# Hybrid layer: zb, o and the mLSTM merge gates by seven products of halves

## The chip, the cores and the metric

The kernel runs on one core of a Trainium2 chip. Its time is the device time of one execution in microseconds (us); the number used is the median of three runs. Engines are called by the profile's names: PE (TensorE, matmuls), ACT (ScalarE), DVE (VectorE), POOL (GpSimd) and SP (SyncE, which issues most DMAs); PEld is PE loading weights.

## The reference, cut to what matters

Two blocks run one after the other on x of 512 tokens by 1024 features, in fp32. The first block (half an FFN, a mixer, half an FFN, a norm) is not touched. The second block is a hybrid layer:

```
h = rms_norm(x, norm_pre_g)
proj = h @ w_in                      # u_a, z_a, q, k, v, o, z_b, gates, g_a, g_b: 1024 columns each, but gates
q, k = silu(depthwise_conv([q, k]))
hb = mlstm_forward(q, k, v) + mlstm_backward(q, k, v)      # 4 heads of 256
y_b = rms_norm_per_head(hb) * sigmoid(o) * silu(z_b)
y_a = (multiscale_pool(u_a) @ pool_mix) * silu(z_a)
merged = sigmoid(g_a + b_merge[0]) * (y_a @ w_proj_pool) \
       + sigmoid(g_b + b_merge[1]) * (y_b @ w_proj_mlstm)
out = x + rms_norm(merged @ w_out, norm_post_g)
```

## The kernel before, in words

All activations are kept transposed: x is eight tiles of 128 features by 512 tokens. To keep fp32 accuracy each operand is held as two parts, hi (a cast by ACT to the fast fp32 format, line 108 for a loaded chunk of weights `raw`, line 177 for anything else) and lo (the rest, a DVE subtraction, lines 109 and 178). One product is three matmuls, hi·hi, hi·lo and lo·hi (`mm3`, lines 125 to 127). Weights come as one stream of chunks of 128 x 1024 in the order of their use: SP loads a chunk into a ring of three `raw` tiles, and its `whi` and `wlo` parts go to rings of three each. A tile of 128 output features is 8 x 3 = 24 matmuls of 512 columns and uses one chunk.

In the FFNs most pairs of gate and up tiles are computed another way (`fast`): the 1024 inputs and the 512 tokens are each cut into two halves, and the 2x2 block product is done with seven products of halves instead of eight, as in Winograd's form of Strassen's method. They are called a, b, p, c, d, f and e, and each is 4 x 3 = 12 matmuls of 256 columns. For that the kernel needs sums of x's halves (`x_sums`: sa, sb, then sxh, sxl) and of the weights' halves: blocks r1, r2, r3 and r4, some of them summed by a DMA that accumulates (POOL's queue), the others by two DVE additions (r<-r,r), and all split into hi and lo. Product a needs r1's parts, p and c those of r2, d and f those of r3, e those of r4. The partial results are put together on the way from the banks fx, fy and fz by ACT copies (fs, fr) and DVE additions (ft, fu). `chain` order: the last two products (f, e) of one pair are placed among the first (a, b) of the next.

The second block runs in this order on PE: the gates' tile; per head q, k, the scores sT and the numerators num, with the values V before heads 0 and 2; eight zb tiles (silu, line 1055) and then eight o tiles (sigmoid, line 1061), whose DVE product lies in `gate`; the transposes hT of the normed heads hb, which DVE multiplies into gate (line 1074), split as ybh and ybl; the merge of branch b (line 1083), in which each mg tile (the gate of the merge, `mgt`) is followed by a pr tile (the projection of y_b); then branch a's u_a, z_a and pooling, its merge, and the output projection. After the last head POOL multiplies the eight x tiles by the row factors r3bc (line 1047), and DVE works out the head norms hrs from hss (lines 202 to 210) and scales hb (line 1067).

What sets the order: the kernel's code gives each operation in sequence, and when the program is built a scheduler fixes each engine's instruction order from it. On the chip each engine goes through its list in order and an instruction waits until its operands, and the tile that it writes, are free. So a late operand holds up everything behind it on its engine. `tc.issue_after` holds the two additions of a fast pair behind a marked instruction. Tiles with one tag share a ring: `big` is a ring of 18 tiles (gate, ybh, ybl and more), and V and PK of the heads and `n2` of the later stages have memory of their own.

Of the kernel before, what the change touches and what calls it, by code (L numbers as in the profile page):

```python
# [44 lines left out]
def kernel(  # L45
# [21 lines left out]
    def wtmp(name, shape=None):  # L67
        return tp.tile(shape or [P, T], F32, tag="w", name=name, bufs=4)
# [155 lines left out]

    def ffn(gname, fstd, ah, al, stats, evac, first=None):
        with tc.tile_pool(name="hp", bufs=2 * max(FPH)) as hp:
# [17 lines left out]

            H = [slice(0, 256), slice(256, 512)]
            sx = []

            def x_sums(k):
                xa, xb = wtmp("xa"), wtmp("xb")
                act.activation(xa, x[k], AF.Copy, scale=vcol(gname, k))  # L250
                act.activation(xb, x[k + 4], AF.Copy, scale=vcol(gname, k + 4))
                h = hp.tile([P, 4, 256], F32R, tag="sx", name="sxh", bufs=8)
                l = hp.tile([P, 4, 256], F32R, tag="sx", name="sxl", bufs=8)
                sa, sb = vtmp("sa"), vtmp("sb")
                dve.tensor_sub(sa[:, H[0]], xa[:, H[0]], xa[:, H[1]])
                dve.tensor_add(sa[:, H[1]], sa[:, H[0]], xb[:, H[1]])
                dve.tensor_sub(sb[:, H[0]], xa[:, H[1]], xb[:, H[1]])
                dve.tensor_sub(sb[:, H[1]], xb[:, H[0]], sa[:, H[1]])
                for j, s in ((0, sa), (2, sb)):
                    split_into(*[m[:, j:j + 2].rearrange("p a b -> p (a b)") for m in (h, l)], s, None)  # L260
                sx.append((h, l))

            for f in range(fstd):
                if first and f == 0:
                    g, u = first
                else:
                    g = gemm_t(tl, ah, al, "g")
                    u = gemm_t(tl, ah, al, "u")
                if rbc is None:
                    rbc = row_bcast(rsqrt_small(sums(stats()), 1.0 / D, "r"))  # L270
                for k in range(KT // 2):
                    if k * fstd // 4 == f:
                        x_sums(k)
                ins = hidden(g, u)
                if f == fstd - 2:
                    marks = [ins]

            def fast():  # L280

                wg, wu = wst[state["n"]], wst[state["n"] + 1]
                state["n"] += 2
                A, B = slice(0, T), slice(T, 2 * T)
                r3 = wp.tile([P, 1024], F32, tag="raw", name="r3", bufs=3)
                r1 = hp.tile([P, 1024], F32, tag="r1", name="r1", bufs=2)
                r2 = hp.tile([P, 1024], F32, tag="r2", name="r2", bufs=2)
                r4 = half("r4")
                nc.sync.dma_start(r3[:, A], wg[:, A])
                nc.gpsimd.dma_start(r3[:, A], wu[:, A], accum_op=ALU.add)  # L290
                nc.sync.dma_start(r4, wu[:, B])
                nc.sync.dma_start(r1[:, A], wg[:, A])
                nc.sync.dma_start(r2[:, B], wu[:, A])
                nc.gpsimd.dma_start(r2[:, B], wu[:, B], accum_op=ALU.add)
                nc.sync.dma_start(r2[:, A], wg[:, B])
                with tc.issue_after(marks[-1].ins):
                    dve.tensor_add(r1[:, B], r3[:, A], r4)
                    dve.tensor_add(r3[:, B], r1[:, B], r2[:, A])
                w = {}
                for r, names in ((r1, "ab"), (r2, "pc"), (r3, "df"), (r4, "e")):  # L300
                    if r is r4:
                        hi, lo = half("hi4", F32R), half("lo4", F32R)
                    else:
                        hi = wp.tile([P, 1024], F32R, tag="whi", name="whi")
                        lo = wp.tile([P, 1024], F32R, tag="wlo", name="wlo")
                    split_into(hi, lo, r, None)
                    for n, c in zip(names, (A, B)):
                        w[n] = hi[:, c], lo[:, c]

                def prod(o, n, xo, start):  # L310
                    for k in range(4):
                        ks = slice(k * P, (k + 1) * P)
                        if isinstance(xo, int):
                            xh, xl = sx[k][0][:, xo], sx[k][1][:, xo]
                        else:
                            p, i = xo
                            xh, xl = ah[k + 4 * p][:, H[i]], al[k + 4 * p][:, H[i]]
                        wh, wl = w[n]
                        for j, (m, v) in enumerate(((wh, xh), (wh, xl), (wl, xh))):
                            pe.matmul(o[:, :256], m[:, ks], v, start=start and k == 0 and j == 0,  # L320
                                      stop=k == 3 and j == 2, skip_group_check=not start)

                X, Y, Z = bank("fx", "mm"), bank("fy", "mm"), bank("fz")
                s1, s2 = wtmp("fs"), wtmp("fr")
                t, u = vtmp("ft"), vtmp("fu")
                prod(X, "a", (0, 0), True)
                act.copy(s1[:, H[0]], X[:, :256])
                yield
                prod(Y, "b", 1, True)
                act.copy(s1[:, H[1]], Y[:, :256])  # L330
                yield
                prod(Z, "p", (1, 0), True)
                dve.tensor_add(t[:, H[0]], Z[:, :256], s1[:, H[0]])
                prod(X, "c", 0, False)
                act.copy(s2[:, H[0]], X[:, :256])
                prod(Y, "d", 2, False)
                dve.tensor_sub(u[:, H[1]], Y[:, :256], s2[:, H[0]])
                yield
                prod(X, "f", (1, 1), False)
                marks.append(dve.tensor_sub(t[:, H[1]], X[:, :256], s1[:, H[1]]))  # L340
                yield
                prod(Y, "e", 3, False)
                dve.tensor_sub(u[:, H[0]], Y[:, :256], s1[:, H[0]])
                hidden(t, u)
                yield

            f0 = fstd
            for ph, n in enumerate(FPH):
                last = None
                for _ in range(f0, n):  # L350
                    g = fast()
                    for i in range(3):
                        next(g)
                        if last and i < 2:
                            next(last)
                    last = g
                for _ in range(2):
                    next(last)
# [543 lines left out]
    big = lambda name, dt=F32, shape=None: bp_.tile(shape or [P, T], dt, tag="big", name=name)  # L902
    lx = ExitStack()
# [49 lines left out]
    def values2(steps=iter(())):  # L953
        V = [[lp.tile([P, 2, 258], F32R, tag="V", name="V", bufs=2 * NT) for _ in range(2)] for i in range(NT)]
# [28 lines left out]
    hb = [lt(f"hb{i}", shape=[P, 2, 256]) for i in range(8)]  # L983
    hss = mb.tile([P, NT, 4], F32, name="hss")
    for h in range(4):
# [18 lines left out]
        PK = [[lp.tile([P, T], F32R, tag="PK", name="PK", bufs=10) for _ in range(2)] for _ in range(5)]  # L1004
# [16 lines left out]
        for t in range(NT):  # L1021
# [19 lines left out]
            sq = mv.tile([P, 256], F32, tag="hsq", name="hsq")  # L1041
            act.activation(sq, hv, AF.Square, accum_out=hss[:, t, h:h + 1])
# [5 lines left out]


    gate = []  # L1050
    for c in range(KT):
        o = gemm_t(tl, ah, al, "zb")
        g = big("gate")
        dve.tensor_mul(g, o, rbc)
        act.activation(g, g, AF.Silu)
        gate.append(g)
    for c in range(KT):
        o = gemm_t(tl, ah, al, "o")
        t = wtmp("og")
        dve.tensor_mul(t, o, rbc)  # L1060
        act.activation(t, t, AF.Sigmoid)
        dve.tensor_mul(gate[c], gate[c], t)
# [17 lines left out]
    np2 = ctx.enter_context(tc.tile_pool(name="n2", bufs=26))  # L1080
    nn = lambda name, dt=F32, shape=None: np2.tile(shape or [P, T], dt, tag="n", name=name)


    def merged(yh, yl, br, into):
        for c in range(KT):
            o = gemm_t(tl, ah, al, "mg")
            t = wtmp("mgt")
            dve.tensor_mul(t, o, rbc)
            act.activation(t, t, AF.Sigmoid, bias=vcol("bmerge", 8 * br + c))
            o = gemm_t(tl, yh, yl, "pr")  # L1090
            into(c, t, o)

    mm = []

    def into_b(c, t, o):
        m = nn("mm")
        dve.tensor_mul(m, t, o)
        mm.append(m)

    merged(yh, yl, 1, into_b)  # L1100


# [61 lines left out]
    merged(yh, yl, 0, into_a)  # L1164
# [59 lines left out]
def _stream(i):  # L1224
# [71 lines left out]
    put(t_tiles(zb))  # L1296
    put(t_tiles(o))
# [73 lines left out]
```

## Time and profile before

| what | value |
|---|---|
| median of three runs | 1617.14 us (1617.07 to 1618.35) |
| the profiled execution's own time | 1618.24 us |
| its span, first to last instruction | 1616.5 us |
| PE busy | 1598.9 us (99%) |
| DVE, ACT, POOL busy | 1087.0, 749.2, 136.6 us |
| mean granted TensorE clock | 0.999 of full speed |
| zb tiles, o tiles on PE | 1184.2 to 1241.2 us, 1241.2 to 1284.7 us |
| merge of branch b on PE | 1287.4 to 1376 us |

The profile is of one execution. Busy time is the time in which an engine had at least one instruction at work; matmuls are pipelined, so that one of 0.39 us may be followed by the next after 0.23. The time from one start to the next, the pitch, is what a matmul costs in a full stream. The first zb matmuls are placed among the last head's work, so the zb stretch is longer than eight tiles alone.

### The profile page before, as it was taken

The page shows a single profiled execution, that of the slowest core. Times are in us where ns is not written, and L with a number is a line of the kernel's source. Part 1 is how long each engine was busy: PE and PEld are TensorE (multiplying, and loading weights), DVE is VectorE, ACT ScalarE, POOL GpSimd, SP SyncE. Part 2 cuts the span into 40 slices and gives each one's busy share as a digit, 9 for nine tenths or more (in the row PEclk, how much of TensorE's full clock was granted, in tenths as well). Part 3 has the DMA queues.
Part 4 walks back from the last instruction along what each step waited for, and adds up shares of the span by engine and source line. Part 5 has one row for each costly group of instructions (what it writes and reads, how often), then busy time and mean ns, then how long its engine had stood idle before and what let it go on. Part 6 is the DMA issues. An engine that isn't in the chain of part 4 may idle for free.

```text
span 1616.5 us, 23488 instructions
## 1 busy us (share of the span) xinstructions
PE 1598.9 (99%) x9050; PEld 1388.9 (86%) x9050; DVE 1087.0 (67%) x1902; ACT 749.2 (46%) x1173; POOL 136.6 (8%) x253
## 2 busy tenths in 40 slices
PE   8999999999999999999999999999999999999997
PEld 6989989987788898898998998888888888888886
DVE  6866866876364866875686778798677543566454
ACT  6533535545244554653352556577573322333341
POOL 0101101000100110110110100011002000110000
PEclk9999999999999999999999999999999999999999
DMA  7545745432142100674574642222222232323231
GB/s 237 142 141 136 188 127 148 133 103 92 53 130 87 34 25 27 151 176 130 138 181 125 162 119 91 92 66 66 65 66 92 78 104 94 100 93 104 92 118 53
DMA packets 68320, 176.22 MB, mean 109 GB/s; under 512 B 7664, under 2 KB 7984, under 8 KB 68208
## 3 DMA queue, kind: packets, MB, share of 16 engines
q1 hardware_dynamic: 56592, 153.38, 29.2%
q0 software_dynamic: 11040, 20.45, 8.0%
q8 instruction: 71, 1.16, 0.3%
q10 hardware_dynamic: 576, 0.89, 0.2%
q14 instruction: 41, 0.34, 0.1%
HBM read 171.55 MB, written 2.10 MB: 107 GB/s over the span
## 4 chain that ended last, share of the span: by engine, by line
PE 94%; DVE 2%; issue 1%; ACT 1%; DMA 0%; POOL 0%; SPq 0%; DVEq 0%; ACTq 0%; POOLq 0%
PE fx L320 10%; PE fy L320 10%; PE dn L127 5%; PE dn L125 5%; PE dn L126 5%; PE fz L320 3%; PE pv L777 2%; PE gn L125 2%; PE gn L126 2%; PE gn L127 2%; PE g L127 2%; PE g L125 2%; PE mg L125 2%; PE mg L126 2%; PE mg L127 2%; PE pr L125 2%
## 5 line engine op out<-in xcount | busy, mean ns | idle before, releaser
L108 ACT CAST whi<-raw 128x1024 fp32r<-128x1024 f32 x179 | 188.0, 1051 | 354.6 <-issue 147.8
L109 DVE TENSOR_TENSOR wlo<-raw,whi 128x1024 fp32r<-128x1024 f32 x179 | 223.5, 1249 | 69.2 <-ACT whi L108 67.5
L177 ACT CAST whi<-r 128x1024 fp32r<-128x1024 f32 x111 | 116.4, 1051 | 115.9 <-PE dn L126 52.8
L178 DVE TENSOR_TENSOR wlo<-r,whi 128x1024 fp32r<-128x1024 f32 x111 | 135.2, 1219 | 15.5 <-ACT whi L177 15.3
L127 PE MATMUL dn<-hdh,wlo 128*128 128x512 f32 x352 | 137.0, 389 | 0.0
L126 PE MATMUL dn<-hdl,whi 128*128 128x512 f32 x352 | 137.0, 389 | 0.0
L125 PE MATMUL dn<-hdh,whi 128*128 128x512 f32 x352 | 136.7, 389 | 0.0
L320 PE MATMUL fx<-xh,whi 128*128 128x256 f32 x296 | 84.3, 285 | 0.0
L320 PE MATMUL fy<-sxh,whi 128*128 128x256 f32 x296 | 83.8, 283 | 0.0
L320 PE MATMUL fy<-sxl,whi 128*128 128x256 f32 x296 | 83.8, 283 | 0.0
L320 PE MATMUL fy<-sxh,wlo 128*128 128x256 f32 x296 | 83.8, 283 | 0.0
L320 PE MATMUL fx<-xh,wlo 128*128 128x256 f32 x296 | 83.7, 283 | 0.0
L320 PE MATMUL fx<-xl,whi 128*128 128x256 f32 x296 | 83.7, 283 | 0.0
L126 PEld LDWEIGHTS dn<-hdl,whi 128*128 128x128 f32 x352 | 66.1, 188 | 13.9 <-DVE hdl L178 0.3
L127 PEld LDWEIGHTS dn<-hdh,wlo 128*128 128x128 f32 x352 | 66.1, 188 | 13.5
L125 PEld LDWEIGHTS dn<-hdh,whi 128*128 128x128 f32 x352 | 66.1, 188 | 13.2
L364 DVE TENSOR_TENSOR dnr<-dn,rbc 128x512 f32<-128x512 f32 x48 | 33.1, 690 | 58.4 <-PE dn L127 58.3
L125 PE MATMUL g<-xh,whi 128*128 128x512 f32 x152 | 61.1, 402 | 6.8 <-ACT xh L180 6.8
L126 PE MATMUL g<-xl,whi 128*128 128x512 f32 x152 | 60.8, 400 | 0.5 <-DVE xl L181 0.5
L127 PE MATMUL g<-xh,wlo 128*128 128x512 f32 x152 | 60.5, 398 | 0.0
L125 PE MATMUL gn<-whi,xh 128*128 128x512 f32 (+1 forms) x160 | 59.1, 370 | 0.0
L127 PE MATMUL gn<-whi,xl 128*128 128x512 f32 (+1 forms) x160 | 59.0, 368 | 0.0
(497 smaller groups left out, 4581.5 us busy)
## 6 DMA issues: line engine op xcount, KB each, us to landing
raw<-in_dram SPq DMA_DIRECT2D x192, 512.0 KB, 3.4
r<-in_dram SPq DMA_DIRECT2D x185, 256.0 KB, 3.6
r<-in_dram POOLq DMA_DIRECT2D x74, 256.0 KB, 4.6
x<-in_dram SPq DMA_DIRECT2D x8, 256.0 KB, 6.5
out_dram<-xn SPq DMA_DIRECT2D x8, 256.0 KB, 2.2
post<-in_dram ACTq DMA_DIRECT2D x2, 256.0 KB, 4.0
acc<-kcT POOLq DMA_DIRECT2D x2, 128.0 KB, 3.2
acc<-vcT POOLq DMA_DIRECT2D x2, 128.0 KB, 2.5
```

Of the source, the lines that this page charges most:

```text
L108: act.copy(hi, raw)
L109: dve.tensor_sub(lo, raw, hi.bitcast(F32))
L125: pe.matmul(out, lh, rh, start=start, stop=False)
L126: pe.matmul(out, lh, rl, start=False, stop=False)
L127: pe.matmul(out, ll, rh, start=False, stop=stop)
L177: act.copy(h, src)
L178: dve.tensor_sub(l, src, h.bitcast(F32))
L320: pe.matmul(o[:, :256], m[:, ks], v, start=start and k == 0 and j == 0, stop=k == 3 and j == 2, skip_group_check=not start)
L364: dve.tensor_mul(t, o, rbc)
L777: pe.matmul(o[:, i * 65:(i + 1) * 65], pt[:, q0:q0 + P], vn[kt][:, b, e, :65], start=(kt == 0), stop=(kt == i))
```

## The change

`seven` (the former `fast`), `x_sums` and `chained` become common functions, and the second block uses them: zb and o are taken in pairs (zb tile c with o tile c). Pairs 0 and 1 stay standard, pairs 2 to 7 go by seven products in one chain. In the merge of branch b the eight mg tiles become four pairs by seven products, each a chain of its own, followed by its two pr tiles. `branch_gate` now does silu and sigmoid for a pair at a time. The sums of x for the second block are made beside the first two pairs (eight sx tiles of each part); since they read x, the row broadcast of r3 and POOL's eight multiplications of x move behind the zb/o chain. One ring `n2` of 26 tiles now holds V, hb and PK of the heads and later sx, the merge's r2a and r2b, mm and the rest. The blocks r2a, r2b, r4 and the parts hi4, lo4 of the zb/o chain, and r4 of the merge, are tiles of `big`. The separate tile hsq goes. The weight stream is packed in the new order. The program has 362 more matmul instructions (84 for 48 in each of ten pairs, and two more).

```diff
+    def seven(ah, al, sx, blocks, marks, done):
+        wa, wb = wst[state["n"]], wst[state["n"] + 1]
...
+        r3 = wp.tile([P, 1024], F32, tag="raw", name="r3", bufs=3)
+        r1, r2, r4, low = blocks()
...
+        nc.sync.dma_start(r4, wb[:, B])
...
+        with tc.issue_after(marks[-1].ins):
+            dve.tensor_add(r1[:, B], r3[:, A], r4)
+            dve.tensor_add(r3[:, B], r1[:, B], ra)
...
+    def branch_gate(z, o):
+        g = big("gate")
+        dve.tensor_mul(g, z, rbc)
+        act.activation(g, g, AF.Silu)
+        t = wtmp("og")
+        ins = dve.tensor_mul(t, o, rbc)
+        act.activation(t, t, AF.Sigmoid)
+        dve.tensor_mul(g, g, t)
...
+    def blocks():
+        r1 = wp.tile([P, 1024], F32, tag="raw", name="r1", bufs=3)
+        return r1, (big("r2a"), big("r2b")), big("r4"), lambda: (big("hi4", F32R), big("lo4", F32R))
+
+    def blocks_b():
+        r1 = wp.tile([P, 1024], F32, tag="raw", name="r1", bufs=3)
+        return r1, (nn("r2a"), nn("r2b")), big("r4"), lambda: [
+            wp.tile([P, 1024], F32R, tag=t, name=t)[:, :T] for t in ("whi", "wlo")]
+
+    for c in range(2):
+        z = gemm_t(tl, ah, al, "zb")
+        o = gemm_t(tl, ah, al, "o")
+        for k in (2 * c, 2 * c + 1):
+            sx.append(x_sums(k, "pre2", [[nn(n, F32R).rearrange("p (a b) -> p a b", a=2) for n in ("sxh", "sxl")]
+                                         for _ in range(2)]))
+        marks.append(branch_gate(z, o))
+    chained(seven(ah, al, sx, blocks, marks, branch_gate) for _ in range(2, KT))
 
     r3bc = row_bcast(r3)
     for d in range(KT):
         pool.tensor_mul(x[d], x[d], r3bc)
-    gate = []
-    for c in range(KT):
-        o = gemm_t(tl, ah, al, "zb")
...
-    for c in range(KT):
-        o = gemm_t(tl, ah, al, "o")
...
-    merged(yh, yl, 1, into_b)
+    def gates_b(t, o):
+        c = len(mm)
+        for d, m in ((c, t), (c + 1, o)):
+            g, ins = merge_gate(1, d, m)
+            pr = gemm_t(tl, yh, yl, "pr")
+            m = nn("mm")
+            dve.tensor_mul(m, g, pr)
+            mm.append(m)
+            marks.append(ins)
+
+    for c in range(0, KT, 2):
+        chained([seven(ah, al, sx, blocks_b, marks, gates_b)])
```

How this moves instructions is shown at three places. First ACT behind the last head. Before, the zb tiles' weights are cast between the last squares of the head; here is its list:

```order
912 L1039 ACTIVATE ha<-num,dn 128x256
913 L1042 ACTIVATE hsq,hss<-hb_10303 128x256
914 L218 COPY rbc<-bc 128x512
915 L1039 ACTIVATE ha<-num,dn 128x256
916 L108 CAST whi<-raw 128x1024
917 L1042 ACTIVATE hsq,hss<-hb_10305 128x256
918 L1055 ACTIVATE gate<-gate 128x512
919 L108 CAST whi<-raw 128x1024
```

The same place after, with r_12369 the block r1 of the first seven-product pair and r_12368 its r3:

```order
926 L233 ACTIVATE xb<-x_79,vs 128x512
927 L177 CAST sxh<-sa 128x512
928 L1069 ACT_TABLE_LOAD
929 L1069 ACTIVATE gate<-gate 128x512
930 L177 CAST sxh<-sb 128x512
931 L1072 ACT_TABLE_LOAD
932 L1072 ACTIVATE og<-og 128x512
933 L177 CAST sxh<-sa 128x512
934 L177 CAST whi<-r_12369 128x1024
935 L177 CAST sxh<-sb 128x512
936 L177 CAST whi<-r2a 128x512
937 L177 CAST whi<-r2b 128x512
```

The first cast of a weight now stands behind the sums of x and two loads of a function table. Second DVE from the last o tile on. Before, the list runs from the last og to the first weight of the merge that is split behind the heads:

```order
1549 L1060 TENSOR_TENSOR og<-o,rbc 128x512
1550 L1074 SCALAR_TENSOR_TENSOR gate<-hT,vs,gate 128x512 x2
1551 L1062 TENSOR_TENSOR gate<-gate,og 128x512
1552 L178 TENSOR_TENSOR ybl<-gate,ybh 128x512
...
1563 L1074 SCALAR_TENSOR_TENSOR gate<-hT,vs,gate 128x512
1564 L178 TENSOR_TENSOR ybl<-gate,ybh 128x512
1565 L1088 TENSOR_TENSOR mgt<-mg,rbc 128x512
1566 L178 TENSOR_TENSOR ybl<-gate,ybh 128x512
1567 L109 TENSOR_TENSOR wlo<-raw,whi 128x1024 x2
1568 L1097 TENSOR_TENSOR mm<-mgt,pr 128x512
```

After, with r_13310 the block r1 of the first merge pair, r_13309 its r3 and r_13313 its r4:

```order
1626 L1071 TENSOR_TENSOR og<-fu,rbc 128x512
1627 L1112 SCALAR_TENSOR_TENSOR gate<-hT,vs,gate 128x512 x4
1628 L1073 TENSOR_TENSOR gate<-gate,og 128x512
1629 L1112 SCALAR_TENSOR_TENSOR gate<-hT,vs,gate 128x512
...
1635 L1112 SCALAR_TENSOR_TENSOR gate<-hT,vs,gate 128x512
1636 L178 TENSOR_TENSOR ybl<-gate,ybh 128x512 x5
1637 L259 TENSOR_TENSOR r_13310<-r_13309,r_13313 128x512
1638 L260 TENSOR_TENSOR r_13309<-r_13310,r2a 128x512
1639 L178 TENSOR_TENSOR wlo<-r_13310,whi 128x1024
1640 L178 TENSOR_TENSOR wlo<-r2a,whi 128x512
```

The first mg product is made (mgt) before the last ybl in the one; in the other the weights of the first merge product are added and split behind all ybl. Third ACT in the merge of branch b. Before, a turn of it reads:

```order
949 L1089 ACTIVATE mgt<-mgt,vs 128x512
950 L108 CAST whi<-raw 128x1024 x2
951 L1089 ACTIVATE mgt<-mgt,vs 128x512
952 L108 CAST whi<-raw 128x1024 x2
953 L1089 ACTIVATE mgt<-mgt,vs 128x512
```

After, the second merge pair, with r_13512 its r1, r_13511 its r3, r_13515 its r4 and raw the chunks of the pr tiles:

```order
1019 L1123 ACTIVATE mgt<-mgt,vs 128x512 x2
1020 L177 CAST whi<-r_13512 128x1024
1021 L292 COPY fs<-fx 128x256
1022 L295 COPY fs<-fy 128x256
1023 L177 CAST whi<-r2a 128x512
1024 L177 CAST whi<-r_13511 128x1024
1025 L177 CAST whi<-r_13515 128x512
1026 L177 CAST whi<-r2b 128x512
1027 L108 CAST whi<-raw 128x1024
1028 L300 COPY fr<-fx 128x256
1029 L108 CAST whi<-raw 128x1024
```

The casts of r2a, r3, r4 and r2b stand behind the copies of the results of products a and b (fs).

## Rows read from the trace of the kernel before

**Rows 1.** The page: busy us (share of the span); DMA issues, count, KB each, us to landing.

```profile
PE 1598.9 (99%) x9050; PEld 1388.9 (86%) x9050; DVE 1087.0 (67%) x1902; ACT 749.2 (46%) x1173; POOL 136.6 (8%) x253
...
r<-in_dram SPq DMA_DIRECT2D x185, 256.0 KB, 3.6
```

**Rows 2.** Waits of PE: line, what for; us in total, times, longest.

```profile
PE g L125 <- ACT xh L180: 6.8, 2, 6.5
PE g L126 <- DVE xl L181: 0.5, 1, 0.5
```

**Rows 3.** Windows: stretch and its us; busy us of PE, PEld, DVE, ACT, POOL; clock.

```profile
9.00:12.00 3.00, 2.85 (x7) 1.49 (x5) 1.48 (x3) 1.75 (x3) 0.00 (x0) 1.00 1.05 389
50.00:95.00 45.00, 45.00 (x350) 43.57 (x349) 34.99 (x52) 24.40 (x37) 4.92 (x6) 1.00 0.69 187
1213.00:1241.00 28.00, 28.00 (x128) 23.27 (x128) 24.34 (x37) 9.75 (x16) 11.04 (x8) 1.00 0.26 83
1285.00:1376.00 91.00, 91.00 (x418) 75.48 (x417) 41.23 (x50) 27.39 (x34) 0.15 (x2) 1.00 0.29 93
```

**Rows 4.** Timeline of PE, o tiles' first and last matmul: start, us, instruction.

```profile
1241.16 0.39 PE L125 MATMUL o<-xh,whi 128*128 128x512 f32 x1
...
1284.45 0.40 PE L127 MATMUL o<-xh,wlo 128*128 128x512 f32 x1
1284.69 2.92 PE L1072 MATMUL hT<-ident,hb 128*128 128x128 f32 x24
```

**Rows 5.** Timeline of PE, first product of two neighbouring fast pairs of the FFN.

```profile
73.26 0.28 PE L320 MATMUL fx<-xh,whi 128*128 128x256 f32 x1
...
83.34 0.28 PE L320 MATMUL fx<-xh,whi 128*128 128x256 f32 x1
```

**Rows 6.** Lines by form, ACT from 1184 to 1376: busy us, mean ns; idle before.

```profile
L108 ACT CAST whi<-raw 128x1024 fp32r<-128x1024 f32 x33 | 34.7, 1052 | 97.6 <-issue 55.8 <-PE mg L126 31.3 <-PE zb L126 6.2
L177 ACT CAST ybh<-gate 128x512 fp32r<-128x512 f32 x8 | 4.9, 619 | 3.3 <-DVE gate L1074 3.2
L1039 ACT ACTIVATE ha<-num,dn 128x256 f32<-128x256 f32 x4 | 1.8, 474 | 3.4 <-DVE dn L1036 3.4
L1055 ACT ACT_TABLE_LOAD x1 | 1.3, 1283 | 0.0
```

**Rows 7.** Timeline of ACT, two casts back to back.

```profile
1294.84 1.14 ACT L177 CAST ybh<-gate 128x512 fp32r<-128x512 f32 x2
```

**Rows 8.** Lines by form, DVE from 1184 to 1376.

```profile
L109 DVE TENSOR_TENSOR wlo<-raw,whi 128x1024 fp32r<-128x1024 f32 x32 | 40.2, 1259 | 4.8 <-ACT whi L108 3.8
L1074 DVE SCALAR_TENSOR_TENSOR gate<-hT,vs,gate 128x512 f32<-128x512 f32 x8 | 5.9, 744 | 0.0
L178 DVE TENSOR_TENSOR ybl<-gate,ybh 128x512 fp32r<-128x512 f32 x8 | 5.5, 683 | 0.4 <-ACT ybh L177 0.4
```

**Rows 9.** Timeline of DVE behind the last head, from 1214 to 1226.

```profile
1214.15 0.69 DVE L1054 TENSOR_TENSOR gate<-zb,rbc 128x512 f32<-128x512 f32 x1 [0.32 <-PE zb L127]
1214.76 0.47 DVE L1040 SCALAR_TENSOR_TENSOR hb<-num,dn,ha 128x256 f32<-128x256 f32 x1
1215.62 2.37 DVE L109 TENSOR_TENSOR wlo<-raw,whi 128x1024 fp32r<-128x1024 f32 x1 [0.39 <-ACT whi L108]
1217.91 1.26 DVE L202 TENSOR_SCALAR hrsv<-hss 128x16 f32<-128x16 f32 x1
...
1225.46 0.17 DVE L208 TENSOR_TENSOR hrsq<-hrs 128x16 f32<-128x16 f32 x1
```

**Rows 10.** Line 1047: duration ns min/median/max, first and last start us.

```profile
L1047 POOL TENSOR_TENSOR x<-x,rbc x8: 1287/1297/2286, 1214.4 to 1224.1; 128x512 f32<-128x512 f32 x8
```

**Rows 11.** Timeline of PE at the program's start: first and ninth matmul, and the tenth.

```profile
6.53 0.79 PE L125 MATMUL g<-xh,whi 128*128 128x512 f32 x1 [6.53 <-ACT xh L180]
...
11.24 0.61 PE L127 MATMUL g<-xh,wlo 128*128 128x512 f32 x1
12.15 0.50 PE L125 MATMUL g<-xh,whi 128*128 128x512 f32 x1 [0.29 <-ACT xh L180]
```

More of the change, by code (lines that the diff above doesn't have):

```diff
@@ L225, in ffn, with chained @@
+    def chained(tiles):
+        last = None
+        for g in tiles:
+            for i in range(3):
+                next(g)
+                if last and i < 2:
+                    next(last)
+            last = g
+        for _ in range(2):
+            next(last)
     def ffn(gname, fstd, ah, al, stats, evac, first=None):
@@ L242, in hidden, with sx_tiles @@
                 return ins
-            H = [slice(0, 256), slice(256, 512)]
             sx = []
[L248 to L261, printed above, removed]
+            def sx_tiles():
+                h, l = [hp.tile([P, 4, 256], F32R, tag="sx", name=n, bufs=8) for n in ("sxh", "sxl")]
+                return [(h[:, 2 * j:2 * j + 2], l[:, 2 * j:2 * j + 2]) for j in range(2)]
             for f in range(fstd):
@@ L272, in ffn @@
                     if k * fstd // 4 == f:
-                        x_sums(k)
+                        sx.append(x_sums(k, gname, sx_tiles()))
                 ins = hidden(g, u)
@@ L276, in ffn @@
                     marks = [ins]
[L280 to L285, printed above, removed]
+            def blocks():
                 r1 = hp.tile([P, 1024], F32, tag="r1", name="r1", bufs=2)
                 r2 = hp.tile([P, 1024], F32, tag="r2", name="r2", bufs=2)
[L288 to L345, printed above, removed]
@@ L347, in ffn, with fast @@
+                return r1, (r2,), half("r4"), lambda: (half("hi4", F32R), half("lo4", F32R))
+            def fast():
+                return seven(ah, al, sx, blocks, marks, hidden)
             f0 = fstd
             for ph, n in enumerate(FPH):
[L349 to L356, printed above, removed]
@@ L357, in ffn @@
-                for _ in range(2):
-                    next(last)
+                chained(fast() for _ in range(f0, n))
                 f0 = 0
@@ L953, in values2 @@
     def values2(steps=iter(())):
-        V = [[lp.tile([P, 2, 258], F32R, tag="V", name="V", bufs=2 * NT) for _ in range(2)] for i in range(NT)]
+        V = [[nn("V", F32R, [P, 2, 258]) for _ in range(2)] for i in range(NT)]
         for i in range(NT):
@@ L981, in conv @@
         return split(a, None, "qk", big)
-    hb = [lt(f"hb{i}", shape=[P, 2, 256]) for i in range(8)]
+    hb = [nn(f"hb{i}", shape=[P, 2, 256]) for i in range(8)]
     hss = mb.tile([P, NT, 4], F32, name="hss")
@@ L1003 @@
             Mb.append(o)
-        PK = [[lp.tile([P, T], F32R, tag="PK", name="PK", bufs=10) for _ in range(2)] for _ in range(5)]
+        PK = [[nn("PK", F32R) for _ in range(2)] for _ in range(5)]
         for j in range(NT):
@@ L1079, with merge_gate @@
     lx.close()
[L1080 to L1091, printed above, removed]
-    mm = []
[L1095 to L1098, printed above, removed]
-    merged(yh, yl, 1, into_b)
+    def merge_gate(br, c, o):
+        t = wtmp("mgt")
+        ins = dve.tensor_mul(t, o, rbc)
+        act.activation(t, t, AF.Sigmoid, bias=vcol("bmerge", 8 * br + c))
+        return t, ins
+    mm = []
+    tl = Tiles()
+    def gates_b(t, o):
[9 more added lines that the diff above has]
+        chained([seven(ah, al, sx, blocks_b, marks, gates_b)])
     yh, yl = [], []
@@ L1162, in into_a @@
         act.copy(xn[i][g], o)
-    merged(yh, yl, 0, into_a)
+    for c in range(KT):
+        t, _ = merge_gate(0, c, gemm_t(tl, ah, al, "mg"))
+        into_a(c, t, gemm_t(tl, yh, yl, "pr"))
     gp2 = []
```

94 lines of the change are left out of this document (81 added, 13 removed).

## The prediction

> **What bounds the kernel now.** I read the page first: TensorE is busy for 99% of the span [rows 1]. Then TensorE's waits: two at the start of the program (6.8 us for the first x tiles, 0.5 us), the largest of six groups that sum to under 9 us in 1616.5 [rows 2]. Then the windows of the stretches that the change touches, and of an FFN stretch that already works by seven products: TensorE is busy for the whole of each, and the vector and scalar engines never fill theirs (VectorE 24.34 of 28 us at most) [rows 3]. So a matmul saved is worth its full pitch, but only as long as TensorE's operands are ready without exception, and any late operand shows at once as new time. The question is not the saving but whether the new order still hides the splitting of the weights.
>
> **1. The products: −8.0 us.** A standard pair of tiles is 48 matmuls of 512 columns. The 192 of the o tiles start from 1241.16 to 1284.45, so (1284.45 − 1241.16)/191 = 0.2266 us each [rows 4], 10.88 us a pair. A pair by seven products is 84 matmuls of 256 columns; in the FFN 84 of them start in 83.34 − 73.26 = 10.08 us [rows 5]. Ten pairs (six zb/o, four mg) save 10 × 0.80 = 8.0 us.
>
> **2. The start of the zb/o chain: +7.7 us.** Call T the end of the last head's last num matmul. After it TensorE has only 5 zb and 24 o matmuls left, 29 × 0.2266 = 6.6 us. In before 11 zb and o tiles with plain loads follow there, whose casts run well ahead. In after the first weight that the chain needs, r1 of the first pair, is cast on ScalarE behind the rest of the head and all of x_sums. By the compiled order that is 4 ha and 4 squares with their reads, 4 xa/xb, 8 sxh casts, 3 table loads, 3 gate functions and the cast itself. Back to back an instruction starts about 0.1 us before its predecessor's end (two ybh casts of 0.62 take 1.14 [rows 7]), so by [rows 6], with a square as a ha and an xa as a cast and a little more, this is 8 × 0.4 + 4 × 0.6 + 8 × 0.52 + 3 × 1.28 + 3 × 0.53 + 1.0 = 16.2 us, of which some 2.5 lie before T. The cast ends at T + 13.7, wlo (1.26 us [rows 8]) at T + 15.0. TensorE's queue holds two product matmuls ahead of the one that needs wlo and is empty by T + 7.3: idle 7.7 us. Bounds: 5 (a third table load or some casts slip behind) and 9.
>
> **3. Between the pairs of that chain: +2 us.** After pair n's d product 19 matmuls (2.3 us) stand before the third a of pair n+1, which needs its wlo. That wlo waits on VectorE for fu<-fy,fr, and its cast on ScalarE for fr, behind two table loads (1.28 each) and two functions of the pair before. In the steady state this just fits (wlo at 1.9 to 2.4 us); the first transitions, where ScalarE still works off x_sums, lack 0.3 to 0.9 each. Bounds 0 and 5.
>
> **4. From the chain's end to the first merge pair: +20 us.** This is the largest term. Let E be the last e matmul. TensorE then has the r3 transposes and 32 hT transposes (24 took 2.92 us [rows 4]; about 4 us in all) and five product matmuls; the sixth waits for wlo of r1. VectorE works first through fu, og, 8 scalings of gate by hT, a gate product, 8 ybl. The DMA that loads r4 of the first merge pair waits for the seventh ybl, because their tiles share the ring of 18. Without disturbance the seventh ybl ends at E + 11.5: 1.0 + 8 × 0.67 of hT scalings + 8 × 0.60 of gate product and seven ybl, by [rows 8, 9] (an operation of 0.69 is followed 0.61 later). r4 needs 3.6 us to land [rows 1]. Then r1's add, cast and wlo follow in a row, 0.68 + 1.05 + 1.26: wlo at E + 18.2, idle 18.2 − 4 − 0.6 = 13.6 us.
> It is disturbed, though. GpSimd's eight products x<-x,rbc stood under zb tiles in before; now they start when rbc is copied, about E + 3. In before, while they ran (8 of 1.3 us, one of them 2.29 [rows 10]), a wlo took 2.37 us instead of 1.26, and six VectorE operations of 16 elements a partition took 1.21 to 1.26 us each, where the same ones took 0.17 as soon as GpSimd had ended [rows 9]. The gate<-zb product, one of whose operands is in PSUM, took its usual 0.69 us there. So each SBUF-only operation seems to take turns with a GpSimd product. The gate product and seven ybl are eight such operations, so each costs a GpSimd product and itself, 1.25 + 0.60 = 1.85 us, with the hT scalings beneath: E + 3 + 8 × 1.85 = E + 17.8 for the seventh ybl, wlo at E + 24.4, idle 20 us. I take 20; bounds 10 (r4 landing while other work remains, no turns) and 21. Nothing covers it: in before the hT transposes stood between mg matmuls whose weights were long split, and here every product after them needs this wlo.
>
> **5. Merge pairs 2 to 4: +6 us.** ScalarE's order puts both fs copies, which wait for product b's end, ahead of the cast of r2a, which product p needs. TensorE is then at p before the cast: a and b last 24 × 0.12 = 2.9 us, the copies and the cast end 1.2 us later (a copy of 256 columns taken a little under a ha [rows 6]), and p's third matmul waits another 0.5 for wlo (0.68). Two pr matmuls stand before f and wait some 0.6 for the cast of their raw tile. That is 2.3 a pair and 6.8 for three; in the fourth eight transposes stand in the gaps, −0.9. Bounds 3 and 8. The first merge pair has its casts in order.
>
> **6. The restart after an idle stretch: +2 us.** At the program's start, after 6.5 us without work, nine matmuls fill the time from 6.53 to 12.15 [rows 11], 0.8 of it waits [rows 2]: 0.53 us each instead of 0.2266, 2.8 us lost. The granted clock is shown as 1.00 there [rows 3], the 2.4 GHz level, so the column doesn't explain it. Two long idle stretches cost 0 to 5.6 us if each ends in such a restart; I take 2. The Trainium skill ("TensorE: Matmul & The Clock Gate", section "What's actually happening") says that an idle array runs at 1.2 GHz until it has been busy for a while. By that rule the full price would fall due twice; the rows' slow pitch agrees with it, their clock column doesn't.
>
> What costs nothing: x_sums on VectorE (it lies in term 2's wait for ScalarE), the shared ring n2 (its tiles are free long before), the last head itself (67 matmuls of cover against 70), and both FFNs and the mixer, whose order is unchanged.
>
> **Sum.** −8.0 + 7.7 + 2 + 20 + 6 + 2 = +29.7 against the profiled execution's own 1618.24 us, which lies 1.1 above the median of the three runs (1617.14). On the median this gives 1647 us, +1.8%. All low bounds together: −8 + 5 + 0 + 10 + 3 + 0 = +10 (1627); all high ones: −8 + 9 + 5 + 21 + 8 + 5.6 = +41 (1658).
>
> **The rivals.**
> - Covered splits (faster). In the FFN stretch the same seven products run at 0.120 us with TensorE busy for 45 of 45 us [rows 3, 5], so the form itself needs no wait. If the weights of both new starts were split in time, only term 1 stays: 1609 us. Against it: in the FFN the first pair's split stands under standard tiles still running, here 6.6 us and 4 us of cover face chains of 15 and 18 to 24.
> - GpSimd doesn't hold VectorE up, as ybl works on other data than the small operations seen: term 4 is 13.6, time 1640 to 1641. For it: only one wide operation was caught in the overlap; against it: that one lost 1.1 us.
> - ScalarE sets the pace of the zb/o chain: two table loads, two functions, five casts and three copies are some 8 us of a pair's 10.08, and if their order makes every transition lack 1.6 us, term 3 is 8: 1653.
> - Both idle stretches end in a restart at the full price of the program's start: term 6 is 5.6, time 1651.
>
> **How the numbers follow.** Chances: my forecast 0.5, GpSimd harmless 0.2, ScalarE's pace 0.1, full restart price 0.1, covered splits 0.05, and 0.05 for a mixture in which some cover that I missed takes most of the 30 us away. Two tenths of a per cent, 3.2 us, is what a measurement can tell from no change. Faster: the covered case, 0.05. Same: half of the last, 0.03. Slower: 0.92. The range, 1630 to 1658, leaves out the covered case and the corner in which every term is at its low end.
>
> **What would show it.** In the profile after, TensorE's waits must list some 7 us for wlo once at the first fx of the chain, 10 to 20 us once after the hT transposes, and two to three waits of 0.5 to 1.2 us in each of merge pairs 2 to 4. Between the waits the 256-column pitch must be 0.120. GpSimd's eight products must lie beside the ybl, and a ybl there must take 1.2 us or more. If TensorE stays busy through both places, the forecast is wrong; if the wait after hT is below 14 us, its turn-taking part is.

## The result, and the profile after

The changed kernel takes 1657.42 us, median of four runs (1655.39 to 1659.21), against 1617.74 before: a ratio of 1.0243, 95% interval 1.0227 to 1.0258. The prediction was 1647 in a range of 1630 to 1658. The profiled execution took 1658.11 us with a span of 1656.4, 39.9 more than before; from the last num matmul to the first ua matmul it is 201.7 us where it was 162.6, so 39.1 of the 39.9 lie in the stretch that the change touches.

The page after shows TensorE busy for longer, 1605.2 us, but for 97% of the span instead of the 99% of [rows 1], and the clock column shows for the first time slices under full speed:

```profile
PE 1605.2 (97%) x9410; PEld 1409.2 (85%) x9410; DVE 1139.0 (69%) x2016; ACT 800.6 (48%) x1262; POOL 156.0 (9%) x273
...
PE   8999999999999999999999999999988599999997
...
PEclk9999999999999999999999999999999799999999
```

TensorE's waits, which were under 9 us in the whole program [rows 2], now read as follows (columns as there):

```profile
PE fx L285 <- ACT whi L177: 21.5, 2, 16.0
PE fx L285 <- ACT fr L300: 6.9, 4, 2.6
...
PE fz L285 <- ACT whi L177: 2.9, 3, 1.0
PE pr L125 <- ACT whi L108: 0.9, 2, 0.4
```

The first line is the two starts (5.5 and 16.0 us), the second the transitions of the zb/o chain, the others merge pairs 2 to 4. In the timeline of PE the start of the chain is one gap, and what follows it is slow:

```profile
1219.73 0.39 PE L127 MATMUL o<-xh,wlo 128*128 128x512 f32 x1
1225.58 0.58 PE L285 MATMUL fx<-xh,whi 128*128 128x256 f32 x1 [5.47 <-ACT whi L177]
...
1230.25 0.41 PE L285 MATMUL fy<-sxl,whi 128*128 128x256 f32 x1
1230.47 0.41 PE L285 MATMUL fy<-sxh,wlo 128*128 128x256 f32 x1
...
1230.88 0.28 PE L285 MATMUL fy<-sxl,whi 128*128 128x256 f32 x1
1231.00 0.28 PE L285 MATMUL fy<-sxh,wlo 128*128 128x256 f32 x1
```

Up to 1230.7 the products start 0.21 us apart, then 0.12 as in the FFN [rows 5]. The windows (columns as in [rows 3]) give the reason in the granted clock, at this place and behind the largest gap:

```profile
1218.00:1226.00 8.00, 2.53 (x12) 1.84 (x11) 7.86 (x20) 7.94 (x13) 0.00 (x0) 0.88 0.23 35
1226.00:1230.00 4.00, 4.00 (x19) 3.88 (x19) 4.00 (x6) 2.93 (x6) 0.00 (x0) 0.50 0.40 126
...
1306.00:1322.00 16.00, 0.48 (x2) 0.48 (x3) 13.50 (x14) 4.05 (x7) 10.46 (x7) 0.60 0.10 33
1322.00:1326.00 4.00, 4.00 (x20) 3.88 (x20) 3.06 (x4) 1.83 (x3) 0.00 (x0) 0.50 0.42 131
```

0.50 is the level of 1.2 GHz. VectorE is busy for 13.50 of the 16 us in which TensorE waits there. Its timeline, and GpSimd's products and the ybl by duration (minimum, median, maximum in ns, as in [rows 10]):

```profile
1304.29 1.02 DVE L1073 TENSOR_TENSOR gate<-gate,og 128x512 f32<-128x512 f32 x1
1305.24 0.74 DVE L1112 SCALAR_TENSOR_TENSOR gate<-hT,vs,gate 128x512 f32<-128x512 f32 x1
1305.90 1.09 DVE L178 TENSOR_TENSOR ybl<-gate,ybh 128x512 fp32r<-128x512 f32 x1
...
1307.57 1.08 DVE L178 TENSOR_TENSOR ybl<-gate,ybh 128x512 fp32r<-128x512 f32 x1
...
1310.91 6.70 DVE L178 TENSOR_TENSOR ybl<-gate,ybh 128x512 fp32r<-128x512 f32 x5
1319.69 0.69 DVE L259 TENSOR_TENSOR r<-r,r 128x512 f32<-128x512 f32 x1 [2.08 <-DMA r<-in_dram]
```

```profile
L1100 POOL TENSOR_TENSOR x<-x,rbc x8: 1277/1708/1712, 1303.5 to 1314.8; 128x512 f32<-128x512 f32 x8
L178 DVE TENSOR_TENSOR ybl<-gate,ybh x8: 678/1090/1747, 1305.9 to 1316.9; 128x512 fp32r<-128x512 f32 x8
```

A ybl takes 1.09 us behind a scaling and 1.75 in a row instead of 0.68 [rows 8]; the last, when GpSimd has ended, takes 0.68 again. Either way one ybl follows the other after 1.67 us, about the time of a product on GpSimd, which takes 1.71 us instead of 1.30. The hT scalings, with one operand in PSUM, keep their 0.74. Behind the ybl r1's addition waits another 2.1 us for the block r4.

The table sets the prediction's terms against the trace. A gap is the time from one matmul's start to the next beyond its pitch; the clock's price is the sum, over windows of 1 us, of PE's busy time times what the granted clock lacks to 1.

| term | predicted | measured |
|---|---|---|
| 1 products | -8.0 | -8.8 (66 matmuls from 1251.86 to 1259.57: 0.119 us each, 84 in 10.0 us) |
| 2 start of the chain | +7.7 | 5.6 |
| 3 inside the chain | +2 | 8.2 (2.7, 1.9, 0.7, 2.3, 0.7) |
| 4 behind the chain | +20 | 17.3 (16.2, and 1.1 among the hT) |
| 5 merge pairs 2 to 4 | +6 | 5.3 (2.1, 2.1, 1.1) |
| 6 clock behind gaps | +2 | 8.3 |
| sum | +29.7 | +35.9 of 39.9 |

The 4 us that are left are not traced one by one; steps of 0.1 to 0.3 us, some 3 us in all, are part of them. The 16.7 us of the expectations below count 0.5 of the steps among the hT with the 16.2.

### The profile page after: what moved, and what is told of

It is laid out like the page before. It is cut to its first block, busy times and chain, and to the rows that moved or that the text cites. A ratio compares the mean times of both kernels' runs of the same rounds, so it can differ in the third digit from the quotient of the medians.

```text
span 1656.4 us, 24572 instructions
## 1 busy us (share of the span) xinstructions
PE 1605.2 (97%) x9410; PEld 1409.2 (85%) x9410; DVE 1139.0 (69%) x2016; ACT 800.6 (48%) x1262; POOL 156.0 (9%) x273
## 5 line engine op out<-in xcount | busy, mean ns | idle before, releaser
L178 DVE TENSOR_TENSOR wlo<-r,whi 128x1024 fp32r<-128x1024 f32 x135 | 162.5, 1204 | 24.2 <-ACT whi L177 23.6
L285 PE MATMUL fx<-xh,whi 128*128 128x256 f32 x376 | 110.0, 293 | 28.5 <-ACT whi L177 21.5
L285 PE MATMUL fy<-sxh,whi 128*128 128x256 f32 x392 | 111.7, 285 | 0.0
L285 PE MATMUL fy<-sxl,whi 128*128 128x256 f32 x392 | 111.6, 285 | 0.0
L285 PE MATMUL fy<-sxh,wlo 128*128 128x256 f32 x392 | 111.4, 284 | 0.0
L285 PEld LDWEIGHTS fx<-xh,whi 128*128 128x128 f32 x376 | 74.2, 197 | 33.1 <-ACT whi L177 22.4
L285 PEld LDWEIGHTS fy<-sxh,whi 128*128 128x128 f32 x392 | 76.2, 194 | 0.0
L285 PEld LDWEIGHTS fy<-sxl,whi 128*128 128x128 f32 x392 | 76.0, 194 | 0.0
L285 PEld LDWEIGHTS fy<-sxh,wlo 128*128 128x128 f32 x392 | 75.8, 193 | 0.0
L285 PEld LDWEIGHTS fx<-xh,wlo 128*128 128x128 f32 x376 | 74.0, 197 | 0.8 <-DVE wlo L178 0.7
L285 PEld LDWEIGHTS fx<-xl,whi 128*128 128x128 f32 x376 | 74.2, 197 | 0.4
```

The costliest lines, as they stand in the source:

```text
L178: dve.tensor_sub(l, src, h.bitcast(F32))
```

## The experiments

Beside each time stands the stretch from the last num to the first ua matmul (before 162.6, after 201.7), since the program around it can vary by some us from run to run. Where more zb and o matmuls stand ahead of the last num (70 before, 67 after), the stretch reads shorter by 0.23 us for each; this is said where it matters.

**The two halves apart.** In one kernel only zb and o go by seven products, in the other only the merge gates.

```diff
-    for c in range(0, KT, 2):
-        chained([seven(ah, al, sx, blocks_b, marks, gates_b)])
+    for c in range(KT):
+        g, _ = merge_gate(1, c, gemm_t(tl, ah, al, "mg"))
+        pr = gemm_t(tl, yh, yl, "pr")
...
-    chained(seven(ah, al, sx, blocks, marks, branch_gate) for _ in range(2, KT))
+    for c in range(2, KT):
+        marks.append(branch_gate(gemm_t(tl, ah, al, "zb"), gemm_t(tl, ah, al, "o")))
```

> zb and o as in the change, the merge of branch b by standard tiles (mg and pr tile by tile, their chunks in the order of before). Theory (each part costs what its own gaps cost): -4.8 of products, +5.6 start, +8.2 in the chain, about 6 of the clock falls there, and behind hT 0 to 5, since mg's plain chunks can be loaded and split early while the ybl still take turns with GpSimd's products: about 1635 (1631 to 1640). Rival (the chain's end itself makes the 17 us, whatever product stands behind): 1648 or more.

> All eight zb/o pairs standard (zipped as in the change, x_sums beside the first two), the merge gates by seven products as in the change. Theory: -3.2 of products, +16.7 behind hT, +5.3 in merge pairs 2 to 4, +2.5 of the one clock fall: about 1639 (1634 to 1643). Rival (the gap behind hT is owed to the late end of the zb/o chain): the gap is under 5 us and the time 1620 to 1628.

zb and o alone: 1638.30 us (1.0121, 1.0104 to 1.0137), stretch 180.5, so +17.9. The merge gates alone: 1643.72 (1.0152, 1.0130 to 1.0175), stretch 184.1, so +21.5. Their sum, 39.4, is close to the whole change's 39.1: the halves cost on their own and neither needs the other for it. Behind hT standard mg tiles leave a wait of 3.7 us, products of halves one of 12.1 even where all zb and o tiles are standard:

```profile
PE hT L1110 <- DVE gate L1112: 3.7, 1, 3.7
```

```profile
PE fx L285 <- ACT whi L177: 12.1, 1, 12.1
...
PE hT L1111 <- DVE gate L1113: 2.9, 1, 2.9
```

The first is the kernel with standard merge tiles, the second the one with standard zb/o. Both theories were met, the second's time missed by 0.7 us above its range: the part ahead of the stretch, which is not changed, was 5.9 us longer in its profile (last num at 1218.8).

**GpSimd's products moved.**

```diff
     chained(seven(ah, al, sx, blocks, marks, branch_gate) for _ in range(2, KT))
-    r3bc = row_bcast(r3)
-    for d in range(KT):
-        pool.tensor_mul(x[d], x[d], r3bc)
...
     for c in range(0, KT, 2):
         chained([seven(ah, al, sx, blocks_b, marks, gates_b)])
+    r3bc = row_bcast(r3)
+    for d in range(KT):
+        pool.tensor_mul(x[d], x[d], r3bc)
```

> The broadcast of r3 and GpSimd's eight products x<-x,rbc are moved behind the whole merge of branch b. Theory (VectorE and GpSimd take turns on the ybl): a ybl takes 0.68 instead of 1.1 to 1.3 us, the seventh ends 4 to 5 us earlier, the gap behind the hT transposes falls from 16.7 to about 12, time about 1652 to 1653. Rival (GpSimd only lies beside it, the r4 transfer sets the gap): the gap stays within 1 us of 16.7, about 1657.

Each ybl takes 0.68 us again, and the gap behind hT fell from 17.3 us to 12.4, as turn-taking said, but the time missed the theory's: it is 1656.00 (1.0229, 1.0212 to 1.0246), stretch 200.5, no different from the change: GpSimd's products now end late for the xn transposes, which the scheduler had put into the fourth merge pair, and a further clock fall follows that wait.

```profile
L178 DVE TENSOR_TENSOR ybl<-gate,ybh x8: 678/680/683, 1304.5 to 1313.3; 128x512 fp32r<-128x512 f32 x8
```

```profile
PE fx L285 <- ACT whi L177: 16.1, 2, 10.7
...
PE xn L1200 <- POOL x L1140: 3.3, 3, 1.9
```

The longest wait for whi is 10.7 now, of 16.0 before the move; 3.3 us came back as a wait for x. The mechanism is shown; the gain was given back.

**The block r4 in another ring.**

```diff
-        return r1, (nn("r2a"), nn("r2b")), big("r4"), lambda: [
+        return r1, (nn("r2a"), nn("r2b")), nn("r4"), lambda: [
```

> The block r4 of the merge pairs is a tile of the ring n2 instead of the ring of 18 that holds the yb parts, so its load need not wait for the seventh ybl; the scheduler then puts r1's addition before the hT scalings and its wlo between the ybl. Theory (the load and VectorE's list behind it make the gap): the gap behind hT falls from 16.7 to 7 to 10 us, about 1649. Rival (VectorE's list alone, the load is hidden): the gap falls by no more than the 2.6 us of the load's landing, 1654 to 1656.

1659.29 us (1.0256, 1.0240 to 1.0271), stretch 201.4. The gaps behind hT fell from 17.3 to 11.2 us (9.5 and 1.7): more than the rival allowed, less than the theory said, and the time lies above both. But the later merge pairs now gap by 3.5, 3.2 and 2.8 us instead of 2.1, 2.1 and 1.1, and the clock fell there twice more (its price 11.2 us instead of 8.3). What is left of the gap behind hT is VectorE's list, in which wlo of r1 stands between the ybl: it is the 9.3 us of the second line, while the first holds the chain's start (5.4) and the starts of merge pairs 2 to 4:

```profile
PE fx L285 <- ACT whi L177: 13.7, 4, 5.4
PE fx L285 <- DVE wlo L178: 10.3, 4, 9.3
```

**Dead matmuls in the gap.**

```diff
     lx.close()
+    o = bank("dead")
+    for i in range(60):
+        pe.matmul(o, ah[i % KT][:, :P], ah[0], start=True, stop=True)
```

> Sixty dead matmuls of 512 columns (13.6 us at full pitch) into a bank that nobody reads are put between the hT transposes and the first merge pair, where TensorE sits idle for 16.7 us. Theory (the idle stretch itself halves the clock, and the restart is paid at 0.213 us a matmul of 256 columns): the stretch behind shows a granted clock of 1.00 and 0.12 us from the first product on, 2 to 2.5 us are saved, about 1655.0. Rival (the slow pitch behind the gap comes from operands that arrive late): the pitch stays, time 1657 or more.

The window behind the gap and the first products in the timeline:

```profile
1320.00:1324.00 4.00, 2.36 (x17) 2.16 (x18) 3.62 (x5) 3.19 (x5) 0.00 (x0) 1.00 0.16 51
```

```profile
1322.37 0.28 PE L285 MATMUL fx<-xh,whi 128*128 128x256 f32 x1
1322.48 0.27 PE L285 MATMUL fx<-xl,whi 128*128 128x256 f32 x1
```

The clock stays at 1.00 and the pitch is 0.12, but for the step right behind a wait (0.23). So the theory's mechanism holds and the rival is out, but the saving is smaller than it said. Behind the hT transposes the clock's price falls from 2.5 us to nothing, and yet the time from the last hT to the first ua falls only from 109.7 to 108.7 us: product a now waits 0.8 us for wlo, which in the change came under the slow products. The stretch as a whole falls from 201.7 to 199.5 and the clock's price in it from 8.3 to 4.7, but the rest of both lies ahead of the dead matmuls, in a chain that the edit doesn't touch and in which the clock fell once less. The time, 1657.26 us (1.0238, 1.0223 to 1.0253), can't be told from the change's.

**One function table.** In the loop of the gates silu(z) becomes z times its sigmoid.

```diff
-        act.activation(g, g, AF.Silu)
+        s = wtmp("og")
+        act.activation(s, g, AF.Sigmoid)
+        dve.tensor_mul(g, g, s)
```

> The silu of zb is computed as zb times its sigmoid, so that ScalarE needs one function table for the whole zb/o and merge stage; VectorE gets one more product of 512 columns for each zb tile. Theory (table loads set the transitions of the zb/o chain: fr, which f's bank waits for, and the cast of r1 stand behind two loads of 1.28 us): the gaps of TensorE inside the chain, 8.2 us in all, fall to 2 or less, the gap at the chain's start from 5.6 to about 3, and two or three of the clock falls go; about 1645 us (1640 to 1649). Rival (the casts, or the landing of the blocks r4, set the transitions): gaps of 6 to 8 us remain in the chain, 1653 to 1658.

1652.85 us (1.0211, 1.0190 to 1.0231), stretch 194.1, of which 1.4 us less than in the change because six more zb and o matmuls stand ahead of the last num. The time lies between theory and rival. No table load is left in the stretch (15 in the change); the gaps in the chain fell from 8.2 to 5.2 us and no clock fall was left inside it, but the start kept its gap (6.1), against the theory. So the table loads don't hold the start. Of the transitions they hold a part; how large it is can't be read off, since VectorE got one more product for each pair.

**The gate functions one step later.** The pair's done (silu, sigmoid and their products) is run behind the next pair's first three steps, and that of the last standard pair behind the first chain pair's.

```diff
+    def chained_later(last, tiles):
+        for g in tiles:
+            for _ in range(3):
+                next(g)
+                next(last)
+            last = g
...
+    chained_later(std_later(z, o), (seven(ah, al, sx, blocks, marks, branch_gate, True) for _ in range(2, KT)))
```

> As the change, but the gate functions of a zb/o pair (silu, sigmoid and their products) are issued one step later, behind the next pair's first products, and those of the second standard pair behind the first chain pair's weights; so fr and the cast of r1 stand before the table loads in ScalarE's list. Theory (the place of the gate functions in ScalarE's list makes the gaps): the gaps inside the chain fall from 8.2 to 2 or less, the start gap from 5.6 to about 2, of the clock falls only the one behind hT and perhaps the first stay; about 1643 (1639 to 1648). Rival (ScalarE's and VectorE's load as a whole is too high for a pair in 10 us): the gaps move elsewhere in the chain and 6 us or more remain, 1652 to 1657.

1647.24 us (1.0181, 1.0158 to 1.0204), stretch 191.4. The start came down to 2.9 us, the gaps behind the chain to 13.1, the clock's price to 5.9. The time lies in the theory's range, but the theory's gaps inside the chain, 2 us or less, did not come: they stayed at 7.1 with other releasers, as the rival said (whose time, 1652 to 1657, was missed). In two of them ScalarE itself stood 1.8 and 2.0 us for the block r4 ahead of a table load, as in the last line, so late blocks have a share:

```profile
PE fy L285 <- DVE fu L302: 2.1, 2, 1.5
PE fx L285 <- ACT fs L292: 2.0, 1, 2.0
PE fx L285 <- DVE wlo L178: 1.4, 3, 1.0
```

```profile
1263.99 0.62 ACT L177 CAST hi<-r 128x512 fp32r<-128x512 f32 x1 [1.81 <-DMA r<-in_dram]
```

**Towards a version that gains.** Three standard pairs, five by seven products with the gates one step later, standard merge tiles, GpSimd's products issued one for each merge tile; then the same with one function table; then with the first mg tile ahead of the hT transposes and GpSimd's products marked to follow the mm products.

> Three standard zb/o pairs and five by seven products with the gate functions one step later, standard merge tiles, GpSimd's eight products x<-x,rbc issued one for each merge tile. Theory (cover at each start, nothing on ScalarE ahead of fr, no turn-taking with the ybl): -4.0 of products, start and chain gaps together under 3, behind hT under 2, no clock fall: about 1616 (1612 to 1622), so the same as before or 0.3% faster. Rival (the start and the end of a chain cost more than five pairs save): 1624 or more.

> The variant with three standard and five seven-product zb/o pairs and standard merge tiles, with zb's silu as zb times its sigmoid. Theory (table loads make its remaining gaps of 7.0 us and the clock fall): gaps of 3 or less, no clock fall, 1618 to 1622. Rival (VectorE sets them): 1625 or more.

> As the variant with three standard and five seven-product zb/o pairs and standard merge tiles, but each of GpSimd's eight products is held behind the product mm of its merge tile (in that variant they ran at the end of the zb/o chain and beside the hT scalings, 1.7 us each), and the first mg tile is issued ahead of the hT transposes. Theory (turn-taking with GpSimd makes the gaps at the chain's end): the gap of 3.0 at hT and the 1.1 us wait for fu go, with them the clock fall of 1.7 to 2.3: 1618 to 1621, no different from before or up to 0.15% slower. Rival (late blocks and ScalarE's list make them): no more than 2 us better than 1625.9.

In all of these, and in the two variants after them, 76 to 78 zb and o matmuls stand ahead of the last num instead of 70, so their stretches read 1.4 to 1.8 us short against before. The first took 1625.94 us (1.0052, 1.0035 to 1.0069), stretch 165.8, on the rival's side: the start's gap is gone, 7.0 us of gaps are left against some 4 saved. With one function table it took 1632.47 (1.0088, 1.0071 to 1.0105), stretch 170.7, again on the rival's side: ScalarE's table loads don't set what is left here. The longest waits are 4.1 us for VectorE's gate products at hT (2.8 in the first) and 2.6 for a copy fs, behind which VectorE had waited 3.9 us for a block to land; so VectorE's list is a part of it, and late blocks are another. The last took 1627.31 (1.0055, 1.0041 to 1.0068), stretch 167.0. It doesn't test what it was made for: the mark orders the list and is no wait on the chip, and GpSimd's products ran in the chain's last pairs as in the first of the three:

```profile
L1167 POOL TENSOR_TENSOR x<-x,rbc x8: 1389/1744/2275, 1278.8 to 1291.4; 128x512 f32<-128x512 f32 x8
```

What turn-taking costs in this variant stays open.

**One chain of nine pairs.** zb/o pairs 3 to 7 and the four mg pairs in one chain, the hT tiles among the last three, the pr tiles behind; with silu, and with one table.

```diff
+    for ht, g in tiles():
+        for _ in range(3):
+            next(g)
+            next(last)
+            if ht:
+                next(ht, None)
+        last = g
```

> One chain of nine pairs: zb/o 3 to 7 and then the four mg pairs, all by seven products, with each pair's gate functions one step later; three standard zb/o pairs before it; the hT tiles one by one among the last three mg pairs; the eight pr tiles behind, with one of GpSimd's products beside each. Theory (no start inside the stage is left without cover): -7.2 of products, some 3 of gaps in the zb/o part as in the three-pair variant with standard merge tiles, 0 to 4 in the mg part, one clock fall at most: 1614 to 1620. Rival (hT scalings and ybl, some 10 us of VectorE, don't fit beside the splits of three pairs): gaps of 8 us or more there and 1624 or more.

> The same, with zb's silu as zb times its sigmoid, so no table load in the chain. Theory (ScalarE's table loads still hold fr and r1's cast in the zb/o part): 1 to 2.5 us less than with silu. Rival (VectorE, which gets 0.6 us more a pair, sets what is left): 0 to 3 us more.

1632.70 us (1.0089, 1.0074 to 1.0104), stretch 173.1, and 1640.30 (1.0137, 1.0121 to 1.0152), stretch 184.1: both misses. The first is as its rival said; the second is slower, as its rival said, but by 7.6 us, not by 0 to 3. Of 15.3 us of gaps in the first, 10 to 12 lie in the mg part; VectorE has little room for the hT scalings and ybl beside the splits:

```profile
1300.00:1350.00 50.00, 41.06 (x284) 38.82 (x283) 43.30 (x57) 25.17 (x42) 16.40 (x13) 0.90 0.39 114
```

VectorE is busy for 43.3 of 50 us there, where a standard merge keeps it at 41.23 of 91 [rows 3]. GpSimd's products lie at the end of the same stretch, so part of this is turn-taking. No variant beat the kernel before.

## Why the prediction came out as it did

The direction, the place and the main mechanism were right: the products save nearly 9 us, and late operands at four kinds of places cost four times that. By term:

**Term 1** held: 0.119 us a matmul at full clock instead of the 0.120 counted, so 0.8 us more saved.

**Term 2** was 2.1 us too high: ScalarE's list ran in the order read, but the cast of r1 ended 12.0 us behind T instead of 13.7, and TensorE began on the cast alone (1225.58); the wlo that I had counted fell under the slow first products.

**Term 3 is the step that failed.** The prediction had the third a wait for its wlo, "In the steady state this just fits". What happens is this, on ScalarE between the second and the third chain pair:

```profile
1245.38 0.62 ACT L177 CAST hi<-r 128x512 fp32r<-128x512 f32 x1 [1.80 <-DMA r<-in_dram]
1246.02 1.28 ACT L1072 ACT_TABLE_LOAD   x1
1247.32 0.63 ACT L1072 ACTIVATE og<-og 128x512 f32<-128x512 f32 x1
1247.85 0.36 ACT L300 COPY fr<-fx 128x256 f32<-128x256 f32 x1
1248.10 1.05 ACT L177 CAST whi<-r 128x1024 fp32r<-128x1024 f32 x1
```

and on PE:

```profile
1245.43 0.28 PE L285 MATMUL fy<-sxh,wlo 128*128 128x256 f32 x1
1248.26 0.58 PE L285 MATMUL fx<-xh,whi 128*128 128x256 f32 x1 [2.55 <-ACT fr L300]
```

Product f adds into the bank fx, which fr must first have copied out. So f, the first thing behind d, waits for ScalarE's list, and none of the 19 matmuls that I had counted as cover can start; four of the five gaps, 6.9 us of wait, end with fr. I had listed fr as a step ahead of the cast, not as what f itself waits for. The FFN has the same copy, but no table loads ahead of it.

In this transition, the longest, ScalarE also stood idle for 1.80 us until the block r4 had landed, ahead of the table load. Without that, fr would have ended that much earlier and some 0.9 of the 2.7 us would be left (an estimate from these lines). In the three later gaps that end with fr no transfer holds ScalarE up: two loads stand before fr there, and short waits for VectorE's products, as at 1269:

```profile
1269.38 1.28 ACT L1072 ACT_TABLE_LOAD   x1 [0.47 <-DVE og L1071]
...
1271.62 0.39 PE L285 MATMUL fx<-xh,whi 128*128 128x256 f32 x1 [1.72 <-ACT fr L300]
```

The rival "ScalarE sets the pace" had the place and the size (8 us; measured 8.2), but one function table took away only 3.0 of these 8.2, and later gate functions only 1.1: fr's place explains most of the waits as they stand, and when it is moved, VectorE's fu and the late blocks are next. How much of the 8.2 each holds is not settled.

**Term 4** was right in mechanism, 17.3 against 20. Turn-taking is shown by the durations and by the move of GpSimd's products (4.9 us of the gap; the prediction's two values differed by 6.4). A ybl alone can take less than the 1.2 us that was asked for as a sign, because a scaling lies between two of them. Two sizes were too large: a turn, 1.67 us and not 1.85, and r4's landing, as r1's addition began 2.7 us behind the seventh ybl and not 3.6. The undisturbed sum was also added up wrongly (1.0 + 8 × 0.67 + 8 × 0.60 is 11.2, not 11.5); the term taken doesn't use it.

**Term 5** was right, 5.3 against 6, by the casts' order as read.

**Term 6** was mis-sized, 8.3 against 2, and over its upper bound of 5.6. I had counted two restarts, at the long gaps, at less than half of their full price. These two alone cost 5.1 us (2.6 and 2.5), near the 5.6 of the rival with the full price. The clock fell four times, and the other two falls, inside the chain behind gaps that term 3 didn't have, cost 3.2. The Trainium skill ("TensorE: Matmul & The Clock Gate", section "What's actually happening") has the array fall to 1.2 GHz when it has been idle. The trace agrees, with 0.50 granted in the windows and 0.21 us a matmul. With dead matmuls in the gap behind hT no fall is left there, so it was the idle stretch and not the late operands that slowed the products.

Terms 3 and 6 were short by 12.5 us, terms 1, 2, 4 and 5 erred the other way by 6.3, and some 4 were not seen: hence 1657 at the range's edge and not 1647. That it still lies in the range owes something to luck, as these errors partly cancel: two rivals that were priced one at a time, ScalarE's pace and the full price of a restart, both came near.

## What to carry to other kernels

On an engine that is busy for 99% of the span, price an edit by what must be ready at each new start, not by its instruction count: here 9 us of saved matmuls bought 36 us of gaps and 8 of a slower clock behind them. When products are chained, list for each the bank that it writes as well as the operands that it reads, and who still has to read that bank. And when work leaves a place where it lay under other work, look at what it meets in the new place, on the other engines as well as in its own queue.

## What the runs showed of the hardware

- The clock at 1.2 GHz outlives the gap: behind the 5.6 us gap some 23 products started mostly 0.21 us apart, until 1230.7, before full pitch came back. Gaps of 16.2, 2.7 and 2.3 us were followed by such a stretch too; one of 1.9 in the same chain was not, nor was one of 3.1 in the kernel with r4 in another ring. So the length of the gap alone doesn't tell.
- VectorE and GpSimd slow each other down, both ways: a ybl takes 1.09 to 1.75 us instead of 0.68, GpSimd's product 1.71 instead of 1.30. The VectorE scalings with an operand in PSUM kept their 0.74.
- At the program's start matmuls of 512 columns come 0.43 us apart or more, 1.9 times the 0.2266 of a full stream, while the column shows 1.00 [rows 3, 11]. Behind the new gaps matmuls of 256 columns come 0.21 us apart, 1.8 times the 0.12, and the column shows 0.50. No run here tells why the column differs.
